# Seven block products for the forget-gate and value projections of a hybrid attention and recurrence block, in a phase of their own

## The chip, the cores and the metric

The kernel runs on one core of a Trainium2 chip. The metric is the device time of one execution in microseconds; the runs give a median. A core has several engines with a queue each: PE multiplies matrices (its weight loads are shown as PEld), DVE works on vectors, ACT evaluates functions, POOL does small jobs, and SP mostly issues transfers. Each engine takes its instructions in a fixed order and waits at one whose inputs are not ready.

## The reference, cut to what matters

One block works on 256 tokens `x` and 256 context tokens `ctx`, 2048 wide. All 512 tokens are normalised and modulated, and go through one wide projection `w_in`. Its columns feed an attention branch and a recurrence branch (16 heads of 128), which are gated, merged and projected out.

```python
xn = rmsnorm(h, norm_gain[l]) * (1.0 + scale) + shift
cn = rmsnorm(hc, norm_gain[l]) * (1.0 + scale_c) + shift_c
aq, ak, av, ag, hq, hff, hfb, hi, hg, ma, mb = split_columns(xn @ w_in[l])
caq, cak, cav, cag, chq, chff, chfb, chi, chg, cma, cmb = split_columns(cn @ w_in[l])
...
def hgrn_forget(z, lb):
    f = lbf + (1.0 - lbf) * jax.nn.sigmoid(z.astype(jnp.float32))
    return to_heads(jnp.log(f)), to_heads(1.0 - f)
...
g_f, k_f = hgrn_forget(hff, lb_f_all[l]);  g_b, k_b = hgrn_forget(hfb, lb_b_all[l])
cg_f, ck_f = hgrn_forget(chff, lb_f_all[l]);  cg_b, ck_b = hgrn_forget(chfb, lb_b_all[l])
v_h = to_heads(hi);  cv_h = to_heads(chi);  q_h = to_heads(jax.nn.silu(hq))
s_f = hgrn2_final_state(ck_f, cv_h, cg_f)                     # the context's state, and backward
o, _, _ = hgrn2_bidir(q_h, v_h, k_f, g_f, k_b, g_b, s_f, s_b)  # forward and backward recurrence
hg_branch = hgrn_readout(o, hgrn_norm_gain[l], hg)            # rmsnorm per head, times silu(hg)
...
y = sigmoid(m_a + b_m[0]) * (hg_branch @ w_o_hgrn) + sigmoid(m_b + b_m[1]) * (att_branch @ w_o_attn)
h = h + gate * (y @ w_out)
```

The forget gates (`hff`, `hfb`) and the values (`hi`) are needed for all 512 tokens, as are the attention's keys and values; the other columns for the 256 tokens of `x` alone.

## The kernel before, in words

**Projections.** Everything is float32. A product is made of three: the weights and the tokens are split into a high part in a shorter format and the rest, and `mm3` (L83 to L85) adds high × high, high × rest and rest × high. `xH` and `xL` hold the split tokens, transposed: 16 slices of 128 features by 512 tokens. A weight chunk of 512 KB is loaded by SP into `raw` (four buffers, L66), copied by ACT to `wh` (L76) and subtracted by DVE into `wl` (L77), three buffers of each. Such a chunk feeds 12 or 24 matmuls, and it is the unit in which a projection is handed out. `proj_col_g` gives 256 columns of weights, transposed, for 512 tokens (a forget gate of two heads: 96 matmuls of 512 columns); `proj_tok_g` gives 512 columns for two or four tiles of 128 tokens (values: four tiles, 192 matmuls of 512); `proj_col_x_g` gives the recurrence's queries.

**Recurrence.** The 16 heads are done as eight pairs by `pair`, a generator. It starts with scans over the forget gates (DVE L525, L526, L529), goes through the levels of products inside the tokens (`A`, `al`, `grow`, `keep`), and ends thus: PE makes `al` (L711), DVE makes the end states from it (L716), PE makes `ob` (L728 to L730), ACT squares it (L736), POOL takes the root (L181, L182), DVE multiplies by gate and root (L740), and PE transposes the result as `to` (L748). These last transposes are put off into the next pair (`done`); ahead of them the next pair's scans are already written down. `X` is a single buffer that both pairs use.

**The order.** PE's order is written out by hand. `weave` takes from a filler of projection steps as much as each `yield` of the pair asks for: 8.5 steps of 24 matmuls in all, and lets the filler run to its end before the next pair. The filler of pair n is `inputs(n + 1)`: the next pair's forget gates, values, output gate and queries; that of the last pair is three merge projections. `with_gates` adds one gate chunk (`gate_chunk`: a 512 KB load of `w_ada`, two L196 on DVE into the sum `acc`) for each three steps of 24 matmuls of filler. There are four groups of eight, each ended by transposes on PE (`tqg`, L202) and a reduction on DVE (L204), all into the same `acc`; what is not yet done after the last pair is done by a loop of 33 steps. Next come `part_a` (the recurrence's output projection, `w_o_hgrn`) and the attention, with its K and V projections. SP's queue has its loads in the order in which the program asks for chunks. DVE, ACT and POOL are ordered by a scheduler from priorities.

Of the kernel before, what the change touches and what calls it, by code (L numbers as in the profile page):

```python
# [7 lines left out]
F32 = mybir.dt.float32  # L8
F32R = mybir.dt.float32r
# [29 lines left out]
def block_kernel(ctx: ExitStack, tc: tile.TileContext, x, c, cx, c_ctx, w_ada, b_ada, norm_gain, w_in,  # L39
# [167 lines left out]

    def forget(banks, d, h0, F):
        for i in range(2):
            sg = base.tile([P, 512], F32, tag="sm", name="sg", bufs=3)  # L210
            act.activation(sg, banks[i], AF.Sigmoid)
            dve.tensor_scalar(F[:, i, :], sg, lbc[:, 2 + d, h0 + i: h0 + i + 1],
                              lbc[:, d, h0 + i: h0 + i + 1], op0=ALU.mult, op1=ALU.add)
# [2 lines left out]
    cg = pad.tile([P, KT], F32, name="cg")  # L216
    gcol = few.tile([P, KT], F32, name="gcol")
    gate_rows = dram.tile([KT, P], F32, name="gate_rows")

    FIRST = (("F0", 2), ("F1", 1), ("F0", 2))  # L220
    with pl("st", reuse_waits="tile") as st:
# [249 lines left out]
                    if i == 3 and u + 1 < len(UNITS):  # L471
                        first_loads(u + 1, *UNITS[u + 1])
        with tc.manual_schedule(engines={mybir.EngineType.PE, mybir.EngineType.SP}):
            first_f = [fp.tile([P, 2, 512], F32, tag=tg, name="ff", bufs=nb) for tg, nb in FIRST]
            with tc.high_priority(2 * PRIO):
                for b, (d, h0) in enumerate(((0, 0), (1, 0), (0, 2))):
                    forget(first[b], d, h0, first_f[b])
            hi = proj_tok_g(w_in, C_HI, x_st, range(4))
            bv0 = result(hi)
# [3 lines left out]
        dve.tensor_copy(mk.rearrange("p a b -> p (a b)"), mkf)  # L483

    biases = {}

# [294 lines left out]
                next(filler, None)  # L781
        run(filler)

    def token_values(bv, grp):
        v = hp.tile([P, 2, 512], F32, tag="v", name="v")
        vc = hp.tile([P, 2, 512], F32, tag="vc", name="vc")
        for t in range(4):
            to_, from_ = (v if t < 2 else vc)[:, t % 2, :], bv[t]
            if t % 2:
                dve.tensor_copy(to_, from_)  # L790
            else:
                act.activation(to_, from_, AF.Copy)
        grp[:2] = [v, vc]

    def output_gate(bg, grp):
        grp[2] = hp.tile([P, 2, 512], F32, tag="gate", name="gate")
        for t in range(2):
            sg = base.tile([P, 512], F32, tag="sm", name="sgg", bufs=3)
            act.activation(sg, bg[t], AF.Sigmoid)
            dve.tensor_tensor(grp[2][:, t, :], bg[t], sg, op=ALU.mult)  # L800

    def gates():

# [12 lines left out]
        while True:  # L816
            yield

    def inputs(n, grp, res):

        g, p = divmod(n, 2)
        h0 = 2 * n
        if n == 1:

            output_gate((yield from proj_tok_g(w_in, C_HG, x_st, range(2))), grp)
        F = [first_f[2] if h0 == 2 and d == 0 else
             fp.tile([P, 2, 512], F32, tag=f"F{d}", name=f"F{d}", bufs=2 - d) for d in range(2)]
        if h0 > 2:
            forget((yield from proj_col_g(w_in, C_FF + h0 * HD)), 0, h0, F[0])
        forget((yield from proj_col_g(w_in, C_FB + h0 * HD)), 1, h0, F[1])  # L830
        if p == 0:
            bv = yield from proj_tok_g(w_in, C_HI + 512 * g, x_st, range(4))
            token_values(bv, grp)
            output_gate((yield from proj_tok_g(w_in, C_HG + 512 * g, x_st, range(2))), grp)
        res[:] = [F, (yield from proj_col_x_g(w_in, C_HQ + h0 * HD))]

    def with_gates(filler):

        for got in filler:
# [2 lines left out]
                count[0] -= 3 * STEP  # L842
                next(gate)
            yield got

    def merge_inputs():
        for n in range(3):
            bm = yield from proj_tok_g(w_in, C_MA + n * 512, x_st, range(2))
            y[n] = fp.tile([P, 2, 512], F32, tag="F0" if n < 2 else "F1", name="y", bufs=2 if n < 2 else 1)
            merge_gate(bm, n, 0, y[n])  # L850

    y = [None] * 4

    def merge_gate(bm, n, row, dst):
        bb = biases.pop((row, n), None)
        if bb is None:
            bb = bias_row(row, n)
        for t in range(2):
            dve.tensor_tensor(dst[:, t, :], bm[t], bb, op=ALU.add)
            act.activation(dst[:, t, :], dst[:, t, :], AF.Sigmoid)  # L860

    with tc.manual_schedule(engines={mybir.EngineType.PE}):
# [3 lines left out]
        token_values(bv0, grps[0])  # L866
        res = [first_f[:2], None]
        res[1] = result(proj_col_x_g(w_in, C_HQ))
        for n in range(8):
            if n == 7:  # L870
                for m in range(2):
                    biases[0, m] = bias_row(0, m, res[0][0][:, 0, 0:1])
# [21 lines left out]
    y[3] = hp.tile([P, 2, 512], F32, tag="vc", name="y")  # L894
    merge_gate(bm, 3, 0, y[3])
    for n in range(1, 4):
        part_a(n)

    XH, XL = xH[:, :, T:], xL[:, :, T:]

    def k_mov(j):
        return XH[:, 2 * j: 2 * j + 2, :], XL[:, 2 * j: 2 * j + 2, :]
# [5 lines left out]
    def split(dh, dl, src, **kw):  # L910
        act.activation(dh, src, AF.Copy, **kw)
        dve.tensor_tensor(dl, src, dh.bitcast(F32), op=ALU.subtract)

    sgb = {}
    Q_TAGS = (("v", "qk"), ("gate", "so"))
# [8 lines left out]
    with tc.manual_schedule(engines={mybir.EngineType.PE}):  # L924
# [1 line left out]
        pool.tensor_copy(sk[:, 0:1], gcol[:, 0:1])  # L926
        nc.gpsimd.dma_start(sk, row_bcast(sink, 16))

        def rope(dst, src, t):

            cos = cs[:, K_COS + t * HD: K_COS + (t + 1) * HD].unsqueeze(1).to_broadcast([P, 4, HD])
            dve.tensor_tensor(dst, src.rearrange("p (h d) -> p h d", h=4), cos, op=ALU.mult)
            tmp = base.tile([P, 4, 2, 2, 32], F32, tag="bb", name="rt", bufs=2)
            sv = src.rearrange("p (h a s d) -> p h a s d", h=4, a=2, s=2)
            sn = cs[:, K_SIN + t * HD: K_SIN + (t + 1) * HD].rearrange("p (a s d) -> p a s d", a=2, s=2)
            for s in range(2):
                dve.tensor_tensor(tmp[:, :, :, s, :], sv[:, :, :, 1 - s, :],
                                  sn[:, :, s, :].unsqueeze(1).to_broadcast([P, 4, 2, 32]), op=ALU.mult)
            tf = tmp.rearrange("p h a s d -> p h (a s d)")
            dve.tensor_tensor(dst, dst, tf, op=ALU.add)  # L940


        bk = proj_tok(w_in, C_K, x_st, range(4))
        kr = at.tile([P, 4, 4, HD], F32, tag="A", name="kr")
        for t in range(4):
            if t < 2:
                rope(kr[:, t], bk[t], t)
            else:
                act.activation(kr[:, t], bk[t].rearrange("p (h d) -> p h d", h=4), AF.Copy)
        bv = proj_tok(w_in, C_V, x_st, range(4))  # L950
        for t in range(4):
            rows = slice(8 + 2 * t, 10 + 2 * t)
            split(XH[:, rows, :], XL[:, rows, :], bv[t].rearrange("p (r c) -> p r c", r=2))

        def keys():
            for z in range(2):
# [142 lines left out]
    for n in range(4):  # L1099
        part_b(n)  # L1100
        if n < 3:
            sgn = gt_tile(n + 1, [P, 2, 512], "sgb")
            merge_gate(sgb[n + 1], n + 1, 1, sgn)
            sgb[n + 1] = sgn
        if n < 2:
            sgb[n + 2] = proj_tok(w_in, C_MB + (n + 2) * 512, x_st, range(2))


    def y_st(kt, t):
# [131 lines left out]
```

## Time and profile before

| | us |
|---|---|
| median of three runs (lowest, highest) | 1630.77 (1630.21, 1631.41) |
| span of the profiled execution | 1629.5 |
| PE busy | 1610.9 |
| PE weight loads busy | 1328.6 |
| DVE busy | 938.3 |
| ACT busy | 762.4 |
| POOL busy | 36.9 |
| mean DMA rate over the span | 168 GB/s |

The span goes from the first to the last instruction of one execution; 1.3 us lie between it and the median. Busy times of different engines overlap. In a row of a group stand line, engine, operation, output and inputs, shape, count, then busy time and mean of one in ns, and the idle time of its engine just before, with what ended it. In a row of the timeline stand start and length in us, and in brackets the idle time before it. In a row of a window stand its ends, then busy time and count of PE, weight loads, DVE, ACT and POOL, the granted PE clock, the DMA engines' busy share and GB/s.

### The profile page before, as it was taken

Reading aid. Unit: us, or ns where it says so; the run is one execution under the profiler, and the core shown is the slowest. Engines: PE = TensorE matmul, PEld = TensorE weight load, DVE = VectorE, ACT = ScalarE, POOL = GpSimd, SP = SyncE. Lnnn points to the kernel's source line nnn. Section 1 sums busy time; section 2 is a strip of 40 time slices with the busy share of each in tenths; the row PEclk is TensorE's granted clock in tenths of the full one; section 3 lists DMA queues with packets and bytes.
Section 4 is the critical chain, followed back from the end, with each engine's and each line's share of the span. In section 5 each row is a group of like instructions: output and inputs, shape, how many; then the busy total and the mean of one; then the engine's idle time right before and its main releaser. Section 6 shows DMA issues by size and latency. Waiting matters only on the chain.

```text
span 1629.5 us, 24667 instructions
## 1 busy us (share of the span) xinstructions
PE 1610.9 (99%) x9882; PEld 1328.6 (82%) x9882; DVE 938.3 (58%) x1464; ACT 762.4 (47%) x1200; POOL 36.9 (2%) x94
## 2 busy tenths in 40 slices
PE   7999999999999999999999999999999999999998
PEld 4668888888888888888888888888888888788887
DVE  4444567546664466645666455335677676555764
ACT  4333455424543345424456443224586786454542
POOL 2000000000000000000000000000000000000000
PEclk9999999999999999999999999999999999999999
DMA  9993544345344553435345555324544454666652
GB/s 368 386 359 129 154 144 143 105 144 189 96 129 130 159 165 104 143 104 188 110 127 171 183 194 194 128 91 145 178 143 143 136 168 155 232 215 205 208 194 91
DMA packets 186690, 274.88 MB, mean 169 GB/s; under 512 B 8624, under 2 KB 105296, under 8 KB 185808
## 3 DMA queue, kind: packets, MB, share of 16 engines
q1 hardware_dynamic: 184032, 266.85, 50.1%
q0 software_dynamic: 1824, 5.35, 1.1%
q8 instruction: 77, 1.26, 0.3%
q10 hardware_dynamic: 720, 1.11, 0.2%
q14 instruction: 37, 0.30, 0.1%
HBM read 271.17 MB, written 2.11 MB: 168 GB/s over the span
## 4 chain that ended last, share of the span: by engine, by line
PE 97%; DVE 1%; issue 1%; ACT 0%; DMA 0%; POOL 0%; POOLq 0%; SPq 0%; ACTq 0%
PE pj L83 24%; PE pj L85 24%; PE pj L84 24%; PE pj L141 7%; PE pj L146 4%; PE pj L409 2%; PE pa L305 2%; PE al L589 1%; PE pj L403 1%; PE pf L409 1%; PE sb L670 1%; PE tkp L1031 1%; PE oba L83 0%; DMA X<-in_x_dram 0%; PE sc L85 0%
## 5 line engine op out<-in xcount | busy, mean ns | idle before, releaser
L77 DVE TENSOR_TENSOR wl<-raw,wh 128x1024 fp32r<-128x1024 f32 x384 | 469.2, 1223 | 400.8 <-ACT wh L76 400.3
L76 ACT ACTIVATE wh<-raw 128x1024 fp32r<-128x1024 f32 x384 | 406.4, 1059 | 581.6 <-PE pj L85 422.1
L84 PE MATMUL pj<-wl,xHL 128*128 128x512 f32 (+1 forms) x1024 | 395.7, 387 | 0.4 <-DVE wl L77 0.4
L85 PE MATMUL pj<-wh,xHL 128*128 128x512 f32 (+1 forms) x1024 | 395.6, 386 | 0.0
L83 PE MATMUL pj<-wh,xHL 128*128 128x512 f32 (+1 forms) x1024 | 391.8, 390 | 0.0
L85 PEld LDWEIGHTS pj<-wh,xHL 128*128 128x128 f32 x1024 | 192.4, 188 | 39.1
L84 PEld LDWEIGHTS pj<-wl,xHL 128*128 128x128 f32 x1024 | 192.6, 188 | 38.2 <-DVE wl L77 0.7
L83 PEld LDWEIGHTS pj<-wh,xHL 128*128 128x128 f32 x1024 | 192.4, 188 | 38.2 <-DVE yt L1087 0.4
L141 PE MATMUL pj<-xHL,wh 128*128 128x512 f32 x512 | 181.1, 396 | 0.0
L83 PE MATMUL pj<-xHL,wh 128*128 128x512 f32 x416 | 164.8, 396 | 0.0
L85 PE MATMUL pj<-xHL,wl 128*128 128x512 f32 x416 | 162.3, 390 | 0.0
L84 PE MATMUL pj<-xHL,wh 128*128 128x512 f32 x416 | 162.1, 390 | 0.0
L146 PE MATMUL pj<-xHL,wl 128*128 128x256 f32 x512 | 139.9, 283 | 0.0
L141 PEld LDWEIGHTS pj<-xHL,wh 128*128 128x128 f32 x512 | 95.1, 188 | 19.1
L84 PE MATMUL pj<-wl,bH 128*128 128x512 f32 x256 | 99.9, 390 | 0.0
L85 PE MATMUL pj<-wh,bL 128*128 128x512 f32 x256 | 99.7, 389 | 0.0
L146 PEld LDWEIGHTS pj<-xHL,wl 128*128 128x128 f32 x512 | 96.7, 189 | 2.5
L85 PEld LDWEIGHTS pj<-xHL,wl 128*128 128x128 f32 x416 | 78.1, 188 | 16.6
L84 PEld LDWEIGHTS pj<-xHL,wh 128*128 128x128 f32 x416 | 78.2, 188 | 15.5
L83 PEld LDWEIGHTS pj<-xHL,wh 128*128 128x128 f32 x416 | 78.2, 188 | 15.5
L83 PE MATMUL pj<-wh,bH 128*128 128x512 f32 x256 | 90.0, 390 | 0.1
L635 DVE TENSOR_TENSOR A<-A,X 128x512 f32<-128x512 f32 x96 | 61.9, 686 | 16.7 <-ACT qk L565 6.7
(289 smaller groups left out, 1690.8 us busy)
## 6 DMA issues: line engine op xcount, KB each, us to landing
raw<-in_w_in_dram SPq DMA_DIRECT2D x300, 512.0 KB, 3.5
raw<-in_w_ada_dram SPq DMA_DIRECT2D x96, 512.0 KB, 7.2
raw<-in_w_o_hgrn_dram SPq DMA_DIRECT2D x32, 512.0 KB, 3.5
raw<-in_w_o_attn_dram SPq DMA_DIRECT2D x32, 512.0 KB, 4.3
raw<-in_w_out_dram SPq DMA_DIRECT2D x28, 512.0 KB, 4.3
X<-in_x_dram SPq DMA_DIRECT2D x2, 1024.0 KB, 6.6
X<-in_ctx_dram SPq DMA_DIRECT2D x2, 1024.0 KB, 10.7
raw<-in_w_in_dram SPq DMA_DIRECT2D x8, 256.0 KB, 7.2
```

The lines of the kernel that those rows point to most:

```text
L76: act.activation(h[:, :n], raw[:, :n], AF.Copy)
L77: dve.tensor_tensor(lo[:, :n], raw[:, :n], h[:, :n].bitcast(F32), op=ALU.subtract)
L83: pe.matmul(o, s[0], m[0], start=first, stop=False)
L84: pe.matmul(o, s[0], m[1], start=False, stop=False)
L85: pe.matmul(o, s[1], m[0], start=False, stop=last)
L141: pe.matmul(banks[i].rearrange("p (a t) -> p a t", a=2), h[:, j, cs_], xHL[:, :, kt, :T], start=kt == 0, stop=kt == KT - 1)
L146: pe.matmul(banks[i][:, :T], lo[:, j, cs_], xH[:, kt, :T], start=False, stop=False)
L305: pe.matmul(pa[32 * g: 32 * g + 32, : 2 * w], cT[:, k0 + g, :], rv_[:, :, g, :], start=k0 == 0, stop=k0 == KT - 4, tile_position=(0, 32 * g))
L403: pe.matmul(o, hw, xL[:, kt, :], start=False, stop=last)
L409: pe.matmul(p_[0], p_[1 + z], xH[:, kt, :], start=kt == 0 and z == 0, stop=False)
L589: pe.matmul(o, ky, mv, start=True, stop=True, tile_position=(0, 32 * g))
L635: dve.tensor_tensor(av, av, f.unsqueeze(3).to_broadcast([P, 2, n2, b]), op=ALU.mult)
```

## The change: a phase ahead of the recurrence

The projection of 2048 features to some columns for 512 tokens is taken as a product of two-by-two blocks: features in two halves, tokens in two halves (of `x` and of the context), weight columns in two halves. By Winograd's form of Strassen's scheme it needs seven block products instead of eight, with sums of blocks on either side. The sums of tokens are made once (`token_sums`, into `S`); the differences of weight blocks are made by DVE for each quad of blocks (`combos`: four subtractions), and seven blocks instead of four are split into `wh` and `wl`. A quad of forget columns (`quad_col`, 13 of them) has 7 × 24 matmuls of 256 columns, a quad of value columns (`quad_tok`, three) 2 × 7 × 24. The partial sums are put together in PSUM, by ACT copies and DVE additions. The first three forget projections and the first value projection stay as they were.

The results are written to device memory by POOL's queue (`F_dr`, `v_dr`), and each pair loads its own. Beside the pairs now run other projections: output gates, seven merge and attention projections (`side_work`; `SIDE` says how many chunks go to each pair) and the queries of the next pair. What they make goes to device memory too, and is loaded at `part_a` and in the attention. After the change a line number of the kernel is higher by 216 in the recurrence (L711 becomes L927, L740 L956, L748 L964).

```diff
+        def combos(b):
+            t = tmp()
+            yield b["11"]
+            sub(t, b["12"], b["11"]);  yield t
+            sub(t, b["22"], t);  yield t
+            yield b["22"]
+            sub(b["12"], b["22"], b["12"]);  yield b["12"]
+            yield b["21"]
+            sub(t, b["21"], t);  yield t
...
+        def quad_col(d, h0):
+            co = (C_FF, C_FB)[d] + h0 * HD
+            b = {n: wload(w_in, 1024 * (n[0] == "2"), 8, (co + HD * (n[1] == "2"),), HD)[0]
+                 for n in ("11", "12", "22", "21")}
+            m_ = [bank8()[:, :T] for _ in range(3)]
+            into = {0: (0, True), 1: (1, True), 2: (0, False), 3: (1, False), 4: (0, False), 5: (2, True), 6: (0, False)}
...
+            for (i, _, mv), src in zip(ORDER, combos(b)):
+                h, lo = [a.rearrange("p (k c) -> p k c", k=8) for a in two(src)]
...
+                    pe.matmul(o, h[:, k, :], mh, start=fresh and k == 0, stop=False, skip_group_check=True)
+                    pe.matmul(o, h[:, k, :], ml, start=False, stop=False, skip_group_check=True)
...
+                    pe.matmul(o, lo[:, k, :], mh, start=False, stop=k == 7,
...
+            nc.gpsimd.dma_start(F_dr[d][h0 // 2], F.rearrange("p i t -> p (i t)"))
...
+            bv0 = proj_tok(w_in, C_HI, x_st, range(4))
...
+            for g in range(2):
+                token_sums(g)
+            for n in range(1, 8):
+                for d in range(2):
+                    if (d, n) != (0, 1):
+                        quad_col(d, 2 * n)
+            for g in range(1, 4):
+                quad_tok(C_HI + 512 * g, v_dr[g])
...
+        for step in ((output_gate(1), merge_out(0, 0), output_gate(2)), (attn_keys(),),
+                     (merge_out(0, 1), output_gate(3), merge_out(0, 2)),
+                     (merge_out(0, 3), merge_out(1, 2), merge_out(1, 3)), (attn_values(),)):
...
+    SIDE = (13, 14, 9, 13, 14, 13, 14, 9)
...
-            weave(pair(n // 2, n % 2, grps[n // 2], *res),
-                  with_gates(inputs(n + 1, grps[(n + 1) // 2], nxt) if n < 7 else merge_inputs()))
+            weave(pair(n // 2, n % 2, grps[n // 2], *res), with_gates(inputs(n, nxt)))
...
-    part_a(0)
-    bm = proj_tok(w_in, C_MA + 3 * 512, x_st, range(2))
+        nc.gpsimd.dma_start(y[n].rearrange("p t c -> p (t c)"), ma_dr[n])
+    for n in range(4):
         part_a(n)
```

Three places show how the instructions move. The first is PE at the end of the last pair. `ob` is the pair's output, `to` its transposes, `tqg` those of a gate group, and `pj` a projection (of `xHL`, the tokens, or of `bH`, the recurrence's output). Before:

```order
L730 MATMUL ob<-so,A 128x128
L728 MATMUL ob<-v,X_7406 128x128
L729 MATMUL ob<-X_7406,A 128x128
L730 MATMUL ob<-so,A 128x128
L83 MATMUL pj<-wh,xHL 128x512
L84 MATMUL pj<-wl,xHL 128x512
L85 MATMUL pj<-wh,xHL 128x512
L83 MATMUL pj<-wh,xHL 128x512
```

And after:

```order
L944 MATMUL ob<-v,X_10559 128x128
L945 MATMUL ob<-X_10559,A 128x128
L946 MATMUL ob<-so,A 128x128
L964 MATMUL to<-cs,so 128x128 x4
L202 MATMUL tqg<-cs,acc 128x128 x4
L83 MATMUL pj<-wh,bH 128x512 x2
L84 MATMUL pj<-wl,bH 128x512
L85 MATMUL pj<-wh,bL 128x512
```

Before, a projection of the tokens follows `ob`, and `to` comes 84 matmuls later; after, `to` and `tqg` follow at once, and then the output projection, which needs them.

The second is SP's queue of loads about the same time. Before:

```order
L66 DMA raw<-in_w_in_dram 128x2x512 x2
L66 DMA raw<-in_w_in_dram 128x4x256 x4
L66 DMA raw<-in_w_ada_dram 128x2x512
L66 DMA raw<-in_w_in_dram 128x4x256 x12
L66 DMA raw<-in_w_in_dram 128x2x512 x24
L66 DMA raw<-in_w_o_hgrn_dram 128x2x512 x8
```

And after:

```order
L66 DMA raw<-in_w_in_dram 128x2x512 x3
L66 DMA raw<-in_w_ada_dram 128x2x512
L66 DMA raw<-in_w_in_dram 128x2x512 x3
L66 DMA raw<-in_w_ada_dram 128x2x512 x11
L66 DMA raw<-in_w_o_hgrn_dram 128x2x512 x32
```

The last gate chunk stood 36 loads of `w_in` ahead of the output projection's weights; now eleven stand in a row right ahead of them.

The third is DVE where one pair ends and the next begins: scans of the next pair, then the product for `so` (that is, for `to`). Before, from the fifth pair to the sixth:

```order
L525 SCALAR_TENSOR_TENSOR X_5670<-F_5052,zero 128x255
L526 SCALAR_TENSOR_TENSOR X_5670<-F_5053,zero 128x255
L529 SCALAR_TENSOR_TENSOR X_5670<-F_5052,X_5670 128x512
L529 SCALAR_TENSOR_TENSOR X_5670<-F_5053,X_5670 128x512
L540 TENSOR_TENSOR qk<-A 128x512
L740 SCALAR_TENSOR_TENSOR so<-ob,ss,gate 128x128 x4
L77 TENSOR_TENSOR wl<-raw,wh 128x1024 x2
```

And after:

```order
L741 SCALAR_TENSOR_TENSOR X_9289<-F_8986,zero 128x255
L742 SCALAR_TENSOR_TENSOR X_9289<-F_8987,zero 128x255
L745 SCALAR_TENSOR_TENSOR X_9289<-F_8986,X_9289 128x512
L745 SCALAR_TENSOR_TENSOR X_9289<-F_8987,X_9289 128x512
L756 TENSOR_TENSOR qk<-A 128x512
L956 SCALAR_TENSOR_TENSOR so<-ob,ss,gate 128x128 x4
L753 TENSOR_TENSOR qk<-qk,hsum 128x256
L196 SCALAR_TENSOR_TENSOR acc<-raw,cg,acc 128x512
```

DVE's order is the same at this place; what stands on PE between `ob` and `to` is not: at this boundary (from the fifth pair to the sixth) 72 matmuls of projection before, 12 after.

More of the change, by code (lines that the diff above doesn't have):

```diff
@@ L473, in block_kernel @@
         with tc.manual_schedule(engines={mybir.EngineType.PE, mybir.EngineType.SP}):
[L474 to L479, printed above, removed]
+            for b, (d, h0) in enumerate(((0, 0), (1, 0), (0, 2))):
+                tg, nb = FIRST[b]
+                ff = fp.tile([P, 2, 512], F32, tag=tg, name="ff", bufs=nb)
+                with tc.high_priority(2 * PRIO):
+                    forget(first[b], d, h0, ff)
+                nc.gpsimd.dma_start(F_dr[d][h0 // 2], ff.rearrange("p i t -> p (i t)"))
             nc.sync.dma_start(cs[:, P:], cst[:, P:])
@@ L799, in output_gate, with merge_out, rope, split @@
             act.activation(sg, bg[t], AF.Sigmoid)
-            dve.tensor_tensor(grp[2][:, t, :], bg[t], sg, op=ALU.mult)
+            dve.tensor_tensor(sg, bg[t], sg, op=ALU.mult)
+            nc.gpsimd.dma_start(hg_dr[g][:, t * 512: (t + 1) * 512], sg)
+    def merge_out(row, n):
+        bm = yield from proj_tok_g(w_in, (C_MA, C_MB)[row] + n * 512, x_st, range(2))
+        bb = bias_row(row, n)
+        for t in range(2):
+            sg = base.tile([P, 512], F32, tag="sm", name="sgm", bufs=3)
+            dve.tensor_tensor(sg, bm[t], bb, op=ALU.add)
+            act.activation(sg, sg, AF.Sigmoid)
+            nc.gpsimd.dma_start((ma_dr, mb_dr)[row][n][:, t * 512: (t + 1) * 512], sg)
+    def rope(dst, src, t):
+        cos = cs[:, K_COS + t * HD: K_COS + (t + 1) * HD].unsqueeze(1).to_broadcast([P, 4, HD])
+        dve.tensor_tensor(dst, src.rearrange("p (h d) -> p h d", h=4), cos, op=ALU.mult)
+        tmp = base.tile([P, 4, 2, 2, 32], F32, tag="bb", name="rt", bufs=2)
+        sv = src.rearrange("p (h a s d) -> p h a s d", h=4, a=2, s=2)
+        sn = cs[:, K_SIN + t * HD: K_SIN + (t + 1) * HD].rearrange("p (a s d) -> p a s d", a=2, s=2)
+        for s in range(2):
+            dve.tensor_tensor(tmp[:, :, :, s, :], sv[:, :, :, 1 - s, :],
+                              sn[:, :, s, :].unsqueeze(1).to_broadcast([P, 4, 2, 32]), op=ALU.mult)
+        tf = tmp.rearrange("p h a s d -> p h (a s d)")
+        dve.tensor_tensor(dst, dst, tf, op=ALU.add)
+    XH, XL = xH[:, :, T:], xL[:, :, T:]
+    def split(dh, dl, src, **kw):
+        act.activation(dh, src, AF.Copy, **kw)
+        dve.tensor_tensor(dl, src, dh.bitcast(F32), op=ALU.subtract)
+    def attn_keys():
+        bk = yield from proj_tok_g(w_in, C_K, x_st, range(4))
+        for t in range(4):
+            kr_ = base.tile([P, 512], F32, tag="sm", name="kr", bufs=3)
+            if t < 2:
+                rope(kr_.rearrange("p (h d) -> p h d", h=4), bk[t], t)
+            else:
+                act.activation(kr_, bk[t], AF.Copy)
+            nc.gpsimd.dma_start(k_dr[:, t * 512: (t + 1) * 512], kr_)
+    def attn_values():
+        bv = yield from proj_tok_g(w_in, C_V, x_st, range(4))
+        for t in range(4):
+            rows = slice(8 + 2 * t, 10 + 2 * t)
+            split(XH[:, rows, :], XL[:, rows, :], bv[t].rearrange("p (r c) -> p r c", r=2))
     def gates():
@@ L817, in gates, with load_forgets, side_work, inputs @@
             yield
[L819 to L835, printed above, removed]
+    def load_forgets(n):
+        F = [fp.tile([P, 2, 512], F32, tag=f"F{d}", name=f"F{d}", bufs=2 - d) for d in range(2)]
+        for d in (1, 0):
+            nc.gpsimd.dma_start(F[d].rearrange("p i t -> p (i t)"), F_dr[d][n])
+        return F
+    def side_work():
+        for step in ((output_gate(1), merge_out(0, 0), output_gate(2)), (attn_keys(),),
+                     (merge_out(0, 1), output_gate(3), merge_out(0, 2)),
+                     (merge_out(0, 3), merge_out(1, 2), merge_out(1, 3)), (attn_values(),)):
+            for g in step:
+                yield from g
+                yield 0
+    side = side_work()
+    SIDE = (13, 14, 9, 13, 14, 13, 14, 9)
+    def inputs(n, res):
+        units, F = 0, None
+        for _ in range(SIDE[n]):
+            got = next(side, None)
+            if got is None:
+                break
+            units += got
+            if F is None and n < 7 and units >= 4 * STEP:
+                F = load_forgets(n + 1)
+            yield got
+        if n < 7:
+            F = F or load_forgets(n + 1)
+            res[:] = [F, (yield from proj_col_x_g(w_in, C_HQ + 2 * (n + 1) * HD))]
+        else:
+            run(side)
     def with_gates(filler):
@@ L844, in with_gates @@
             yield got
[L846 to L850, printed above, removed]
     y = [None] * 4
@@ L927, in block_kernel @@
         nc.gpsimd.dma_start(sk, row_bcast(sink, 16))
[L929 to L943, printed above, removed]
-        kr = at.tile([P, 4, 4, HD], F32, tag="A", name="kr")
[L945 to L953, printed above, removed]
+        kr = at.tile([P, 4, 4, HD], F32, tag="A", name="kr")
+        nc.gpsimd.dma_start(kr.rearrange("p t h d -> p (t h d)"), k_dr)
         def keys():
@@ L1102, in block_kernel @@
             sgn = gt_tile(n + 1, [P, 2, 512], "sgb")
-            merge_gate(sgb[n + 1], n + 1, 1, sgn)
+            if n == 0:
+                merge_gate(sgb[1], 1, 1, sgn)
+            else:
+                nc.gpsimd.dma_start(sgn.rearrange("p t c -> p (t c)"), mb_dr[n + 1])
             sgb[n + 1] = sgn
-        if n < 2:
-            sgb[n + 2] = proj_tok(w_in, C_MB + (n + 2) * 512, x_st, range(2))
     def y_st(kt, t):
```

198 lines of the change are left out of this document (175 added, 23 removed).

## The prediction

> **What bounds the kernel now.** I read the page's busy shares and slices first, then its chain of waits, then the costliest groups.
>
> ```profile
> span 1629.5 us, 24667 instructions
> PE 1610.9 (99%) x9882; PEld 1328.6 (82%) x9882; DVE 938.3 (58%) x1464; ACT 762.4 (47%) x1200; POOL 36.9 (2%) x94
> PE   7999999999999999999999999999999999999998
> DVE  4444567546664466645666455335677676555764
> PEclk9999999999999999999999999999999999999999
> ...
> PE 97%; DVE 1%; issue 1%; ACT 0%; DMA 0%; POOL 0%; POOLq 0%; SPq 0%; ACTq 0%
> ...
> L77 DVE TENSOR_TENSOR wl<-raw,wh 128x1024 fp32r<-128x1024 f32 x384 | 469.2, 1223 | 400.8 <-ACT wh L76 400.3
> ```
>
> PE is the bound from end to end: 99% busy, full in every slice but the first and the last, and 97% of the chain. DVE is at 58%, and its largest group waits for others. So PE time that the change removes comes off one for one, and so does every stall that it adds; there is hardly one to be removed. The span is 1629.5 us and the median of the runs 1630.77, so I add 1.3 us to a span.
>
> **The saving on PE.** A busy time is no pitch, since matmuls overlap. The pitch is read from starts in the timeline of PE, in two unbroken stretches (the first and last row of 24 intervals, then of 23):
>
> ```profile
> 1579.65 0.62 PE L83 MATMUL pj<-wh,xHL 128*128 128x512 f32 x2
> ...
> 1585.09 0.62 PE L83 MATMUL pj<-wh,xHL 128*128 128x512 f32 x2
> ...
> 1599.16 0.28 PE L83 MATMUL pj<-wh,xHL 128*128 128x256 f32 x1
> ...
> 1601.92 0.28 PE L83 MATMUL pj<-wh,xHL 128*128 128x256 f32 x1
> ```
>
> The pitch is 5.44/24 = 226.7 ns at 512 columns and 2.76/23 = 120.0 ns at 256. In the rows of PE's order the change takes 1824 matmuls of 512 columns away and adds 3192 of 256: 1824 × 0.2267 − 3192 × 0.1200 = 413.5 − 383.0, or 30.4 us less. Seven eighths of the arithmetic would have saved more; narrow matmuls give a part of it back, 13.3 ns each over half of the wide one.
>
> [...]
>
> **The ends of the pairs.** Each pair of heads ends in ob, whose results go through squares (ACT), a root (POOL) and a product (DVE L740), and back to PE for the transposes to (L748). DVE has the next pair's scans ahead of that product, and they can't start before ob, since X is one buffer. In the timeline (PE's last ob, then DVE without a gap):
>
> ```profile
> 439.45 0.39 PE L730 MATMUL ob<-so,A 128*128 128x128 f32 x2
> 439.66 0.69 DVE L525 TENSOR_TENSOR_SCAN X<-F,zero 128x255 f32<-128x255 f32 x1
> ...
> 442.00 1.26 DVE L529 SCALAR_TENSOR_TENSOR X<-F,X 128x512 f32<-128x512 f32 x2
> 443.19 0.68 DVE L540 TENSOR_TENSOR qk<-A 128x512 f32<-128x512 f32 x1
> 443.79 1.12 DVE L740 SCALAR_TENSOR_TENSOR so<-ob,ss,gate 128x128 f32<-128x128 f32 x4
> ```
>
> The product ends at 444.91, 5.2 us after ob was done (no later than 439.66, when DVE could start). Before, 11 to 76 us of projection stood on PE between ob and to, so nobody noticed. After, PE's order has 12 matmuls of 512 (12 × 0.2267 = 2.72 us) there at four of the seven boundaries, 24 (5.44 us) at two, 48 at one. PE is in order, so the transposes hold the projection behind them. Stall: 5.2 − 2.72 = 2.5 us, up to 2.9 where a split stands on DVE ahead of the scans, four times 2.7; about 0.6 at the two; none at the last: **+12 us** (10 to 16; it can't be a gain). The projections that stood there are the very ones now done earlier, so no other work takes their place.
>
> **The end of the recurrence.** In the last pair nothing at all is left on PE between al, ob and to. The last pair before, in the timeline, with the group of the gate's chunks and the loads:
>
> ```profile
> 889.01 1.12 DVE L716 SCALAR_TENSOR_TENSOR X<-so,X,al 128x128 f32<-128x128 f32 x4 [0.45 <-PE al L711]
> ...
> 896.72 0.39 PE L730 MATMUL ob<-so,A 128*128 128x128 f32 x2
> 897.14 0.28 ACT L736 ACTIVATE so<-ob 128x128 f32<-128x128 f32 x1 [1.57 <-PE ob L730]
> ...
> 899.72 1.12 DVE L740 SCALAR_TENSOR_TENSOR so<-ob,ss,gate 128x128 f32<-128x128 f32 x4 [2.89 <-POOL ss L182]
> ...
> L196 DVE SCALAR_TENSOR_TENSOR acc<-raw,cg,acc 128x512 f32<-128x512 f32 x60 | 44.9, 748 | 45.8 <-DMA raw<-in_w_ada_dram 45.1
> ...
> raw<-in_w_o_hgrn_dram SPq DMA_DIRECT2D x32, 512.0 KB, 3.5
> ...
> L76 ACT ACTIVATE wh<-raw 128x1024 fp32r<-128x1024 f32 x384 | 406.4, 1059 | 581.6 <-PE pj L85 422.1
> ```
>
> ob waits for L716, 0.45 + 1.12 = 1.5 us after al; to waits for L740, 900.84 − 897.1 = 3.7 us after ob. Then comes what the shorter pairs leave over. Gate chunks are paid out by projection time in the pairs, which is now less: by the order 21 of 32 are done in them, 11 at the end, and SP's queue has all 11 ahead of the first w_o_hgrn weights. acc is one sum, so the eight chunks of the last group start only when the transposes tqg of the group before are over. Each is two L196 of 0.75 us, start to start some 0.67, so 1.34 us; L204 (0.7) goes first. With four raw buffers the first w_o_hgrn load gets that of the fifth chunk: 0.7 + 5 × 1.34 = 7.4 us after tqg, landing 3.5 us later, split on ACT 1.06, and on DVE behind most of the chunks 1.2: PE goes on about 13 us after tqg. The sum is 1.5 + 3.7 + 13.2 = **18.4 us** (14 to 22); before, PE had 196 us of projection there and the chunks long done.
>
> A gap can also cost the clock behind it. After this kernel's own first idle time, the windows (PE, weight loads, DVE, ACT, POOL, granted clock, DMA share, GB/s) show 0.84 and then 0.59:
>
> ```profile
> 18.00:21.00 3.00, 1.66 (x9) 1.30 (x9) 1.61 (x9) 0.03 (x1) 2.38 (x6) 0.84 1.09 385
> 21.00:24.00 3.00, 3.00 (x17) 1.27 (x16) 0.00 (x0) 0.00 (x0) 0.13 (x1) 0.59 1.09 386
> ```
>
> The two stretches are 0.5 and 1.2 us short of full clock, 1.7 us for a long gap, which I leave to the range. [...]
>
> **The new phase.** PE needs 168 × 0.12 = 20.2 us for a forget block. DVE does seven splits, four differences, three sums and two scalings for it:
>
> ```profile
> L1137 DVE TENSOR_TENSOR lw<-lw,gt 128x1024 f32<-128x1024 f32 x4 | 4.9, 1226 | 4.3 <-DMA lw<-in_w_out_dram 4.3
> L156 DVE TENSOR_TENSOR hsum<-pj,hsum 128x256 f32<-128x256 f32 x32 | 13.3, 415 | 0.0
> L212 DVE TENSOR_SCALAR F<-sg,lbc 128x512 f32<-128x512 f32 x26 | 14.1, 544 | 30.4 <-ACT sg L211 30.4
> raw<-in_w_in_dram SPq DMA_DIRECT2D x300, 512.0 KB, 3.5
> 265.00:310.00 45.00, 45.00 (x460) 37.66 (x459) 26.38 (x46) 19.98 (x38) 0.00 (x0) 1.00 0.34 106
> 920.00:960.00 40.00, 40.00 (x178) 33.14 (x177) 19.76 (x18) 15.38 (x15) 0.00 (x0) 1.00 0.60 194
> ```
>
> 11 × 1.225 + 3 × 0.415 + 2 × 0.544 = 15.8 us, under 20.2. A chain remains: block 12 keeps its buffer until its difference is split, then comes the reload, a difference, a split, and a bank that must be read out before product seven writes it. With a landing of 3.5 us I reckon some 1 us of slack. The blocks come in pieces of 512 bytes, which this trace hardly shows. From the two windows, 1 KB pieces (a forget projection) move 106/0.34 = 312 GB/s over 16 engines, 52 ns a piece, and 2 KB pieces 323 GB/s, 101 ns; on that line 512 bytes take some 28 ns, so a load (64 pieces an engine) is no slower. If they cost 52 ns, it takes 64 × 0.052 − 32 × 0.052 = 1.7 us longer: 22 us in 13 blocks. The nearest row is the line's own lower end, so I take the first, with **+4 us** for the starts and the value blocks' halves (0 to 22). The token sums, 43 us of DVE beside 43.5 us of the first value projection on PE, get **+1 us** (0 to 5). The stores and reloads go through POOL, 2% busy, some 90 issues of 0.6 to 0.8 us, and the reloads stand a pair ahead: nothing, while each is covered by a pair's 50 us.
>
> **The pairs themselves.** The last pair before had only 12-matmul chunks beside it, as all have after:
>
> ```profile
> 829.00:895.00 66.00, 66.00 (x582) 56.06 (x581) 48.82 (x78) 41.48 (x74) 3.08 (x8) 1.00 0.54 166
> ```
>
> DVE is busy for 48.8 of 66 us, and PE has no stall. A pair after is some 53 us on PE; 13 us fewer are 4.8 chunks with a split of 1.22 each, so DVE has 48.8 − 5.8 = 43 of 53 us, 81% instead of 74%. The wait that can come is on L196 or a level product late by a split. Nearest is this row, without a stall; the far bound is DVE at 51 of 53 with its chain exposed for 2 to 3 us a pair. I take **+5 us** (0 to 20). K, V and merge projections moved into the pairs keep their matmuls; y, kr and the gates come from memory by loads issued long before: nothing.
>
> **Sum.** −30.4 + 12 + 18.4 + 4 + 1 + 5 = +10.0 us: span 1639.5, median about 1640.8. I forecast 1640. About 0.2%, 3.3 us, is what a measurement tells from no change.
>
> **Rivals.**
> - The tail is short: the last eight gate chunks cost PE nothing, because w_o_hgrn's weights get buffers before them. Then 13.2 us fall away: −3.2, 1627.5, and faster with any other term at its lower end (no wait in the phase: 1623). It decides when the tail's stall is under 5 us. Against it: SP's order has the chunks first, and L196's row shows that DVE takes them at 0.75 us each.
> - Small pieces cost as much as 1 KB ones: +18 on top, 1658. For it: nothing in the trace shows the line going on below 1 KB.
> - DVE bounds the pairs: 20 instead of 5, 1655. For it 81% in a mean; against it the pair without a stall at 74%.
> - Narrow matmuls lose less than the two stretches say, as where each issue costs next to nothing beyond its columns: with the wide pitch simply halved, 113 ns, 51.7 us are saved and not 30.4, 1619. Against it are the 23 equal intervals of 120 ns.
> - That the saving isn't made is no case: the 1824 and 3192 stand in PE's order.
>
> **Chances.** Forecast case (stalls at ends and boundaries as counted) 0.57, short tail 0.12, small pieces 0.13, DVE 0.15, pitch 0.03. Faster: most of the short tail (0.08), the pitch (0.03), and 0.08 of the forecast case with its terms at their lower ends (10 + 14 + 0 + 0 + 0 − 30.4 = −6) make 0.19. Same: 0.03 of the short tail and 0.08 of the forecast case, 0.11. Slower: 0.70. The range goes from 1624, the short tail, to 1662, one of the large bounds with some of the other.
>
> **What the profile after would show.** A pitch of 120 ns in the phase, 20.2 us from one forget block to the next (22 or more: pieces or chain); gaps of 2.5 to 3 us on PE ahead of to at four boundaries, released by DVE's product; one idle time of about 13 us after the last tqg, ended by a weight split; PE's share down to 97%. Wrong if the last is missing, if the boundaries show no gap, or if the gaps in the pairs add up to more than both.

## The result: 2.2% slower, 1666.6 us

| | us |
|---|---|
| before, median (lowest, highest) | 1630.71 (1630.21, 1631.41) |
| after, median (lowest, highest) | 1666.61 (1664.88, 1667.80) |
| ratio, 95% interval | 1.0219 (1.0205 to 1.0233) |
| span of the profiled execution, before and after | 1629.5 and 1666.0 |

The page of the changed kernel, the rows that answer to those shown of before:

```profile
span 1666.0 us, 28103 instructions
PE 1599.0 (96%) x11250; PEld 1379.5 (83%) x11250; DVE 1142.8 (69%) x1677; ACT 844.0 (51%) x1317; POOL 83.6 (5%) x183
...
PE   7999999999999998989989999969999999999998
...
PEclk9999999999999999999999999979999999999999
...
PE 84%; DVE 7%; DMA 4%; issue 2%; ACT 2%; POOL 0%; SPq 0%; POOLq 0%; DVEq 0%; ACTq 0%
...
raw<-in_w_in_dram SPq DMA_DIRECT2D x300, 512.0 KB, 3.6
```

PE is still the bound, but it is no longer full: slices 16 to 27, which are the recurrence and its end, have holes, and one slice has a lower clock. The phase ahead of them has none. Its blocks end at even distances, as the stores of POOL's timeline show, and PE is busy for all of a stretch in it (window: PE, weight loads, DVE, ACT, POOL, clock, DMA share, GB/s):

```profile
299.68 0.53 POOL L627 DMA_DIRECT2D F<-F  x1 [19.63 <-DVE F L625]
319.85 0.53 POOL L627 DMA_DIRECT2D F<-F  x1 [19.63 <-DVE F L625]
...
320.00:340.00 20.00, 20.00 (x169) 20.00 (x169) 15.16 (x16) 9.49 (x13) 0.38 (x1) 1.00 0.43 133
```

20.16 to 20.17 us a block is 168 × 0.120 us: by the phase's pitch the saving on PE came in full. The loads in pieces of 512 bytes stall nothing: the 48 that were issued between 200 and 440 us landed in 3.6 us (median), as did those of the whole tensor, and PE has no wait in the phase. Where the time went is in the list of what PE waited for (sum, count, longest):

```profile
PE to L964 <- DVE so L956: 23.4, 12, 5.0
PE pj L83 <- ACT wh L76: 15.4, 1, 15.4
...
PE tqg L202 <- DVE bL L970: 4.1, 2, 2.9
PE ob L946 <- DVE X L932: 2.3, 3, 1.2
```

Each is a wait at a pair's end or in the tail (from the last pair's `al` on). Before, the same list has no wait ahead of `to`, `tqg`, `ob` or the output projection, and none above 0.5 us behind the kernel's first 35 us. But the waits, 25.6 us at the seven pair ends and 19.6 in the tail, are not all that is lost there. PE's timeline at the fifth pair end:

```profile
905.36 0.33 PE L964 MATMUL to<-cs,so 128*128 128x128 f32 x1 [2.04 <-DVE so L956]
905.88 0.90 PE L964 MATMUL to<-cs,so 128*128 128x128 f32 x3 [0.19 <-DVE so L956]
906.43 0.78 PE L83 MATMUL pj<-wh,xHL 128*128 128x512 f32 x1
907.01 0.63 PE L84 MATMUL pj<-wl,xHL 128*128 128x512 f32 x1
907.43 0.63 PE L85 MATMUL pj<-wh,xHL 128*128 128x512 f32 x1
...
909.68 0.39 PE L85 MATMUL pj<-wh,xHL 128*128 128x512 f32 x1
909.91 0.39 PE L83 MATMUL pj<-wh,xHL 128*128 128x512 f32 x1
```

After this gap of 2 us matmuls start 0.43 us apart, not 0.23, for some 3 us. The windows show it as a granted clock below 1 at this pair end and in the tail (before, it is 1.00 in every stretch of 20 us from 40 to 1620 us):

```profile
900.00:920.00 20.00, 17.77 (x88) 14.72 (x87) 17.07 (x32) 11.85 (x25) 2.58 (x8) 0.91 0.44 136
1080.00:1120.00 40.00, 21.25 (x84) 16.46 (x84) 23.46 (x34) 11.30 (x20) 2.34 (x4) 0.70 0.64 212
```

I measured each pair end from the start of ob to the next `tw` (PE's transposes of the next pair's scans), less what its matmuls take unhindered (ob 2.6 us, a projection by its 0.2267 us, to 0.45), and the slow stretch after tw where one is left: 6.4, 7.7, 3.3, 6.3, 4.3, 5.6, 6.0 us, 39.6 in all; of these 25.6 are waits and 14 slow matmuls. The tail, from al to the second tqg, took 1107.36 − 1075.21 = 32.2 us for 7.6 us of matmuls: 24.6 lost, 19.6 waiting and 5 slow. With −30.4 for the blocks and 1 us of waits inside the pairs that makes +34.8; the spans differ by 36.5. Of the other 1.7 us, 1.0 stands already in the first 62 us, where PE waits somewhat longer for its first loads (the `pa` that starts at 60.64 us before starts at 61.63 us after); the rest is not placed.

### The profile page after: what moved, and what is told of

Same layout as the page of the kernel before. It is cut to its first block, busy times and chain, and to the rows that moved or that the text cites. A ratio compares the mean times of both kernels' runs of the same rounds, so it can differ in the third digit from the quotient of the medians.

```text
span 1666.0 us, 28103 instructions
## 1 busy us (share of the span) xinstructions
PE 1599.0 (96%) x11250; PEld 1379.5 (83%) x11250; DVE 1142.8 (69%) x1677; ACT 844.0 (51%) x1317; POOL 83.6 (5%) x183
## 4 chain that ended last, share of the span: by engine, by line
PE 84%; DVE 7%; DMA 4%; issue 2%; ACT 2%; POOL 0%; SPq 0%; POOLq 0%; DVEq 0%; ACTq 0%
PE pj L83 14%; PE pj L84 13%; PE pj L85 13%; PE pj L141 5%; DMA raw<-in_w_ada_dram 3%; PE pj L601 3%; PE pj L597 3%; PE pj L596 3%; PE pj L146 3%; PE pm L601 3%; PE pm L597 3%; PE pm L596 3%; PE pj L415 2%; DVE wl L77 2%; PE pa L311 2%
## 5 line engine op out<-in xcount | busy, mean ns | idle before, releaser
L83 PE MATMUL pj<-wh,xHL 128*128 128x512 f32 (+1 forms) x832 | 325.3, 396 | 0.0
L84 PE MATMUL pj<-wl,xHL 128*128 128x512 f32 (+1 forms) x832 | 323.7, 389 | 0.0
L85 PE MATMUL pj<-wh,xHL 128*128 128x512 f32 (+1 forms) x832 | 323.0, 388 | 0.0
L85 PEld LDWEIGHTS pj<-wh,xHL 128*128 128x128 f32 x832 | 158.1, 190 | 32.5
L83 PEld LDWEIGHTS pj<-wh,xHL 128*128 128x128 f32 x832 | 158.5, 191 | 30.8 <-ACT sg L211 0.4
L141 PE MATMUL pj<-xHL,wh 128*128 128x512 f32 x512 | 180.9, 395 | 0.0
L141 PEld LDWEIGHTS pj<-xHL,wh 128*128 128x128 f32 x512 | 95.0, 188 | 18.6
L83 PE MATMUL pj<-wh,bH 128*128 128x512 f32 x256 | 92.3, 397 | 15.5 <-ACT wh L76 15.4
L146 PEld LDWEIGHTS pj<-xHL,wl 128*128 128x128 f32 x512 | 96.6, 189 | 3.2 <-DVE wl L77 0.7
L577 ACT ACTIVATE wh<-T 128x1024 fp32r<-128x1024 f32 x57 | 60.3, 1058 | 74.3 <-DVE T L558 22.8
L578 DVE TENSOR_TENSOR wl<-T,wh 128x1024 fp32r<-128x1024 f32 x57 | 69.6, 1220 | 17.6 <-ACT wh L577 17.6
L83 PEld LDWEIGHTS pj<-wh,bH 128*128 128x128 f32 x256 | 48.6, 191 | 26.7 <-ACT wh L76 15.8
L196 DVE SCALAR_TENSOR_TENSOR acc<-raw,cg,acc 128x512 f32<-128x512 f32 x60 | 44.9, 749 | 36.6 <-DMA raw<-in_w_ada_dram 35.9
```

The source lines that it names most:

```text
L83: pe.matmul(o, s[0], m[0], start=first, stop=False)
L84: pe.matmul(o, s[0], m[1], start=False, stop=False)
L85: pe.matmul(o, s[1], m[0], start=False, stop=last)
L141: pe.matmul(banks[i].rearrange("p (a t) -> p a t", a=2), h[:, j, cs_], xHL[:, :, kt, :T], start=kt == 0, stop=kt == KT - 1)
L146: pe.matmul(banks[i][:, :T], lo[:, j, cs_], xH[:, kt, :T], start=False, stop=False)
L577: act.activation(h, src, AF.Copy)
```

## The experiments

Theory 1: the loss is PE waiting for DVE at the pair ends and for the gate chunks in the tail. Theory 2, which goes with it: the gaps also cost slow matmuls. The main rivals: DVE is simply too busy in the recurrence, so that moving one wait makes another; the reloads from device memory delay things; the seven products don't save what they should. Each ran against the kernel before on the same chip, whose median was 1630.65 both times.

**The put-off transposes later.** `e1_to_after_tw` moves three lines of `pair`.

```diff
-        for f in done:
-            f()
-        done[:] = []
         yield 0.5
         wT = X2[:, 1024:].rearrange("p (a s) -> p a s", a=8)
...
         yield 1.0
+        for f in done:
+            f()
+        done[:] = []
         so = hp.tile([P, 2, 512], F32, tag="so", name="so")
```

> The put-off transposes `to` stand after the next pair's `tw` and 24 more matmuls, just ahead of sb. Theory 1 (PE waits at the pair ends for DVE's product, and each such gap also lowers the clock): at the seven pair ends of the changed kernel some 39 us are lost; now `tw` is what PE waits for, and only the two ends whose scans are behind a gate chunk still wait. About 14 us stay lost there, the tail stays as it is: 1666.6 - 26 = 1641 us (1633 to 1650), and hardly a wait of PE `to`. Rival (DVE is short of time in the pairs, so its lateness shows up at whatever comes next, tw or sb): within 5 us of 1666.6.

Measured: 1641.3 us (1639.6 to 1642.3), ratio 1.0062 (1.0047 to 1.0077). What PE waits for now:

```profile
PE pj L83 <- ACT wh L76: 15.7, 1, 15.7
...
PE tw L872 <- DVE X L745: 6.4, 3, 2.8
PE to L964 <- DVE so L956: 3.3, 2, 3.1
```

The 23.4 us of `to` are 3.3 (those of the tail), and 6.4 are at tw at the second and seventh pair end. 25 us came back: DVE is late at the pair ends, not short of time in the pairs, and the rival falls.

**The gate chunks in the phase.** `e2_gates_in_phase` loads them into the idle buffer of F1, one ahead of and one within each forget block, the last six within the value blocks, and sums the four groups in the two halves of acc in turn.

```diff
-        wr = wload(w_ada, k0 * P, 2, (4096 + 512 * g,), 512)[1][:, 0]
+        wr = fp.tile([P, 2, 512], F32, tag="F1", name="gr", bufs=1)
+        nc.sync.dma_start(wr, w_ada[k0 * P: (k0 + 2) * P, 4096 + 512 * g: 4608 + 512 * g]
...
+        def pay():
+            if paid[0] < 32:
+                g, k = divmod(paid[0], 8)
+                gate_chunk(accT[:, g % 2, :], g, 2 * k)
+                paid[0] += 1
...
-            weave(pair(n // 2, n % 2, grps[n // 2], *res), with_gates(inputs(n, nxt)))
+            weave(pair(n // 2, n % 2, grps[n // 2], *res), inputs(n, nxt))
```

> All 32 gate chunks are taken in the phase ahead of the recurrence, into a buffer of their own (the one of F1, idle there), two a block; none is left in the pairs or the tail. Theory 1 with the gate chunks as the reason of the tail (25 us lost with the slow clock behind it) and of the long waits at the second and the seventh pair end: the tail loses 2 us instead of 25, the pair ends about 18 less, the phase at most 6 more: 1627 us (1618 to 1640). Rival (the reloads from device memory, not the chunks, make DVE late at the pair ends): only the tail is saved, 1643 us.

Measured: 1634.9 us (1631.1 to 1637.1), ratio 1.0023 (1.0014 to 1.0033). PE's waits:

```profile
PE to L980 <- DVE so L972: 9.6, 8, 2.4
...
PE pj L608 <- DVE sg L626: 5.6, 5, 2.6
PE pj L608 <- ACT wh L579: 3.2, 2, 2.2
```

The 15.4 us wait of the tail is gone, and so are the waits ahead of `to` at the second and the seventh pair end; what is left is 2.0 to 2.4 us at four pair ends, just the ends with 12 matmuls. In exchange the phase, with 1.34 us more on DVE for each chunk, stalls for some 11 us. The reloads are all still there, so the rival (1643) falls too; the time alone, half way between the two forecasts, would not show it, the waits do.

The edit changed more than I had written: PE's order in the tail is another. The output projection of the finished heads now stands between the last pair's ob and to:

```profile
1070.94 0.39 PE L961 MATMUL ob<-so,A 128*128 128x128 f32 x2
1071.08 0.48 PE L83 MATMUL pj<-wh,bH 128*128 128x512 f32 x1
...
1086.35 0.40 PE L83 MATMUL pj<-wh,bH 128*128 128x512 f32 x1
1086.58 0.27 PE L980 MATMUL to<-cs,so 128*128 128x128 f32 x1
```

So the tail's 0.9 us ahead of ob and 3.3 us ahead of to went as well. The same order stands in `e6_chunks_in_pairs`, `e12_both`, `e15_spread` and `e16_no_phase_chunks`, whose tails have no gate chunks either.

Why a chunk made a pair end longer is seen in DVE's timeline of the changed kernel, at the second one (ob is done at 709.5):

```profile
710.12 0.41 DVE L753 TENSOR_TENSOR qk<-qk,hsum 128x256 f32<-128x256 f32 x1
714.03 0.75 DVE L196 SCALAR_TENSOR_TENSOR acc<-raw,cg,acc 128x512 f32<-128x512 f32 x1 [3.51 <-DMA raw<-in_w_ada_dram]
714.70 0.68 DVE L741 TENSOR_TENSOR_SCAN X<-F,zero 128x255 f32<-128x255 f32 x1
...
719.82 1.12 DVE L956 SCALAR_TENSOR_TENSOR so<-ob,ss,gate 128x128 f32<-128x128 f32 x4
```

DVE stands for 3.5 us at a gate chunk whose load has not landed, with the scans and the product for `to` behind it. PE had 24 matmuls here, and still waited 5.0 us.

**The clock by itself.** `e3_keep_warm` puts transposes of the identity, whose results nobody reads, ahead of each `to`.

```diff
+            warm = ps.tile([P, 512], F32, tag="tp", name="warm")
+            for q in range(24):
+                pe.transpose(warm[:, (q % 4) * P: (q % 4 + 1) * P], ident, ident)
             to = ps.tile([P, 2, 2, HD], F32, tag="tp", name="to")
```

> 24 idle transposes of the identity stand ahead of each `to`, some 2.6 us of PE at full clock; nobody reads them. Theory 2 (a gap of 2 to 5 us on PE costs as much again as slow matmuls after it, some 2.2 us at each pair end): the gaps are filled by work of no use, the waits for DVE stay, and 12 us of slow clock fall away: 1654 us (1648 to 1660), with the granted clock near 1.00 behind the first seven pair ends. Rival (the clock falls for another reason, such as the load itself): no gain, 1666 to 1672, clock as low as now.

Measured: 1656.7 us (1655.8 to 1657.1), ratio 1.0156 (1.0139 to 1.0173): 10 us less with 192 instructions more. The windows around the fifth pair end and the seventh:

```profile
900.00:920.00 20.00, 20.00 (x223) 16.85 (x222) 14.73 (x26) 11.86 (x18) 1.70 (x3) 1.00 0.68 211
...
1010.00:1030.00 20.00, 19.94 (x117) 17.74 (x115) 15.36 (x31) 9.75 (x23) 1.99 (x6) 0.92 0.41 134
```

The clock is 1.00 in the windows at the first six pair ends (at the third it was so already); at the seventh it still falls, to 0.92, where PE waits 2.4 us in ob, ahead of the idle work. At the other five, where the changed kernel's windows have 0.91 or 0.92, the gap, once filled, no longer lowers it: there it was the gap that did.

But a gap doesn't always do it. In the changed kernel and in `e4_plain_phase` (below) PE waits the same 2.94 us ahead of the same tqg, at the third pair end; the 6 us behind it, in the one and in the other:

```profile
791.38:797.38 6.00, 6.00 (x33) 5.17 (x34) 3.52 (x9) 3.49 (x6) 1.32 (x2) 1.00 0.59 174
...
819.03:825.03 6.00, 6.00 (x21) 5.25 (x22) 2.99 (x8) 2.39 (x5) 1.32 (x2) 0.51 0.62 177
```

In `e2_gates_in_phase` two gaps of 2.05 us ahead of to were followed by 1.00 (at 670 us) and by 0.72 (at 907 us). In the recurrences of these runs a single gap of 0.8 to 1.8 us left the clock at 0.98 to 1.00 in the 6 us behind it, and each of 3 us or more lowered it (in the changed kernel 3.21 us to 0.72, 4.03 to 0.72, 5.03 to 0.61, 15.41 to 0.50); between, neither length nor place decides, and what does stays open.

**The seven products undone.** `e4_plain_phase` keeps the phase, the stores and the reloads, and makes the blocks with `proj_col_g` and `proj_tok` (eight block products, no token sums).

```diff
-                        quad_col(d, 2 * n)
+                        banks = result(proj_col_g(w_in, (C_FF, C_FB)[d] + 2 * n * HD))
...
+                            forget(banks, d, 2 * n, F)
...
-                quad_tok(C_HI + 512 * g, v_dr[g])
+                bv = proj_tok(w_in, C_HI + 512 * g, x_st, range(4))
```

> The phase, its stores and reloads, and all else stay, but the 13 forget blocks and three value blocks are made as before by eight block products (matmuls of 512 columns), without the token sums. Theory 1 (the seven products save on PE what was counted): 13 x 1.6 + 3 x 3.2 = 30.4 us more, 1697 us (1693 to 1701). Rival (the narrow matmuls and DVE's extra work eat the saving): at most 10 us more, under 1677.

Measured: 1693.6 us (1688.8 to 1697.7), ratio 1.0383 (1.0361 to 1.0405). 27.0 us more than with seven products, where 30.4 were counted; the highest run is 31 over the changed kernel's median, the lowest 22, so the difference of 3 is not settled. The saving is real. PE's waits, and the busy shares:

```profile
PE to L972 <- DVE so L964: 20.6, 12, 3.8
PE pj L83 <- ACT wh L76: 16.0, 1, 16.0
...
PE 1633.0 (96%) x9882; PEld 1341.0 (79%) x9882; DVE 935.4 (55%) x1464; ACT 763.0 (45%) x1200; POOL 83.2 (5%) x183
```

The waits for `to` and in the tail are there as well, with DVE at 55%: they come with the new order of the recurrence, not with the seven products.

**All chunks in the pairs.** `e6_chunks_in_pairs` changes one number.

```diff
-            if count[0] >= 3 * STEP:
-                count[0] -= 3 * STEP
+            if count[0] >= 15 * STEP // 8:
+                count[0] -= 15 * STEP // 8
```

> Gate chunks are paid out for each 1.875 steps of projection instead of 3, so that all 32 are taken in the pairs; `to` stays where the change has it. Theory 1 (the tail is lost to the chunks that stand in front of w_o_hgrn's weights): the tail's 25 us shrink to about 1; half again as many chunks stand on DVE in the pairs, and where one waits for its load ahead of the scans, a pair end gets longer, 5 us in all: 1648 us (1640 to 1656). Rival (the tail waits for w_o_hgrn's loads themselves or for the last product, whoever stands before them): 1660 or more.

Measured: 1645.8 us (1643.3 to 1648.0), ratio 1.0091 (1.0075 to 1.0108). The tail's wait is gone altogether; PE's wait for `to` is 17.1 us, 7.8 the longest. So the tail's long wait was the chunks in front of w_o_hgrn's weights (here too the output projection moved in between ob and to), and chunks in the pairs make the scans late.

**Together.** `e12_both` is the first two edits; `e15_spread` is the same with one chunk in a forget block, three or four in a value block and the last eight in the pairs; `e16_no_phase_chunks` is the edit of `e1_to_after_tw` with that of `e6_chunks_in_pairs`.

> Both edits together: `to` behind tw, and all gate chunks in the phase. Theory 1: of the kernel with the chunks in the phase (1634.9), the four waits for DVE's product (2.05 + 2.39 + 2.05 + 2.38 = 8.9 us) and the slow clock behind them (about 8 us) fall away; the phase keeps its 10 us of waits for DVE: 1618 us (1612 to 1624), faster than the kernel before. Rival (DVE's lateness moves on to tw, sb or the levels): 1630 or more.

> As both edits, but one gate chunk in a forget block instead of two, four in a value block, and the last eight in the pairs, one for six steps. Theory 1 with DVE's load as what stalled the phase: its waits go from 10 us to about 2, the pairs keep theirs near 0: 1608 us (1602 to 1616). Rival (it is the shared order on SP or the output of a block that stalls the phase, not the number of chunks): 1615 to 1622.

> `to` behind tw, and all 32 gate chunks in the pairs at 1.875 steps each, none in the phase or the tail. Theory 1: 1641.3 of `to` moved alone, less 24 for the tail, plus 3 to 5 for chunks that make the scans late ahead of tw: 1620 us (1614 to 1628). Rival (DVE is now too full in the pairs): 1635 or more.

| | median (lowest, highest) | ratio, interval |
|---|---|---|
| `e12_both` | 1619.6 (1618.3, 1620.2) | 0.9930 (0.9915 to 0.9945) |
| `e15_spread` | 1616.7 (1615.5, 1618.4) | 0.9914 (0.9899 to 0.9929) |
| `e16_no_phase_chunks` | 1628.0 (1620.0, 1635.2) | 0.9980 (0.9965 to 0.9996) |

All are faster than the kernel before, the second by 14 us, the third by an interval that only just leaves out 1. The recurrence of the changed kernel and that of `e15_spread`, in windows (the second runs 14 us into the output projection):

```profile
564.00:1084.00 520.00, 489.16 (x4408) 411.82 (x4407) 371.86 (x620) 288.95 (x540) 50.39 (x111) 0.98 0.61 200
...
600.00:1080.00 480.00, 478.81 (x4424) 407.47 (x4423) 352.86 (x589) 291.50 (x544) 48.20 (x106) 1.00 0.61 198
```

In the second PE is full and the clock is 1.00, with the reloads and the side work as before: DVE isn't short of time there. I had expected 1608 for `e15_spread`. Its remaining waits in the phase, 8.4 us, lie in the first two blocks and one later; the three longest:

```profile
184.16 1.22 PE L616 MATMUL pj<-S,wl 128*128 128x256 f32 x8 [1.34 <-DVE wl L583]
187.58 0.58 PE L611 MATMUL pj<-S,wh 128*128 128x256 f32 x1 [2.20 <-ACT wh L582]
...
224.35 0.35 PE L611 MATMUL pj<-xHL,wh 128*128 128x256 f32 x1 [2.18 <-DVE sg L629]
```

In DVE's order three chunks stand in the first 20 us, where I had written one, next to the last token sums; and `e12_both`, with twice the chunks in a forget block, has the same waits there. So the rival, that the shared order and not the number matters, is the better account; no run took the order alone. `e16_no_phase_chunks` missed by 8 us and its runs spread over 15: half again as many chunks in the pairs make single waits of up to 4.4 us at ob and 2.2 us at tw.

## Why the prediction was wrong

The direction was right, at +36 us instead of +10; the time lies 5 us above the range. The step that failed is the term for the ends of the pairs, with the slow matmuls behind each gap that the sum left out. By the prediction's own terms:

| term | forecast | measured |
|---|---|---|
| saving on PE | −30.4 | −30.4 by the phase's pitch; 27.0 lost when undone |
| ends of the pairs | +12 | +39.6 |
| end of the recurrence | +18.4 | +24.6 |
| new phase | +4 | 0 |
| token sums | +1 | 0 |
| pairs | +5 | +1 |

The last three terms were 9 us too high, which by luck hid a part of what the two ends were short: 27.6 and 6.2 us.

- **The saving** and **the phase**: right. Matmuls of 256 columns start 0.120 us apart (6.7 ns over half of the 226.7 at 512; the 13.3 of the prediction is for two of them), and the slack that I reckoned in a block was enough. The pieces of 512 bytes landed in 3.6 us: the rival of the small pieces is out, and so is that of the cheaper narrow matmuls.
- **The ends of the pairs**: the step that failed. The mechanism was the one named, at the places named, but it was mis-sized by 28 us, in two parts. The waits are 25.6 us instead of 12: I took DVE's 5.2 us from a pair end of before where nothing was in its way. That price holds where no gate chunk is in the pairs: the four ends that still wait in `e2_gates_in_phase` wait 2.0 to 2.4 us each, and 2.5 to 2.9 were forecast. In the changed kernel DVE comes to the scans 1.1 us late at the first end (a split and the sums of the queries' halves stand ahead), 2.1 us late at the fourth (half a gate chunk and a split) and 4 to 5 us late at the second and the seventh, where a gate chunk waits for its load. I had named L196 as a wait that could come, but inside the pairs, at 5 us. The transposes tqg at the third and the sixth pair end wait another 2.9 and 1.1 us, for L970, which I had not seen: they come after `to` in the same PSUM tag and after only 12 matmuls of projection. At the third end 60 matmuls stood ahead of `to`, not 48, and it had no wait.
- **The slow clock**: the other 14 us at the pair ends and 5 in the tail. I had the row for it (0.84 and 0.59 after the first idle time), priced it at 1.7 us for one gap, and left it to the range. Six pair ends and the tail had it. Idle work ahead of `to` took 10 us of it back. The gap ahead of that row was no long one, as I called it: PE had waited 1.5 us, and then 0.3 (in the changed kernel it is 0.8 and 0.3 there, and the clock stays at 1.00). At the pair ends the shortest gaps that slow matmuls followed were 2.04, 2.38 and 2.67 us, at the fifth, the sixth and the first; with idle work ahead of `to` the clock was 1.00 at all three.
- **The end of the recurrence**: the place and the chain were right (0.9, 3.3 and 15.4 us of waits for the 1.5, 3.7 and 13.2 forecast); the 5 us of slow matmuls are what was mainly missing. The rival of a short tail is out.
- **Stores and reloads cost nothing**: PE waits for none of them in the list above, and `e15_spread`, with all of them, has PE full (478.8 of 480 us).
- DVE as the bound of the pairs, a rival at 20 us, is out as such (1 us of waits inside the pairs): what costs is not DVE's load but the order of what stands in its queue.
- The profile after would show a gap "at four boundaries": they are at six, and two of the three longest waits are at the ends with 24 matmuls of cover. One idle time after tqg, ended by a weight split, came as forecast, at 15.4 us instead of 13.

## What to carry to other kernels

Work that is moved away from a place takes its cover along: for each wait that the moved work hid, count the time that is left, from the worst row of the chain and not from a quiet one, and look at what else stands ahead in the waiting engine's queue, loads above all. On PE, price a new gap like those here, 2.0 to 5.0 us, at its length and some 2 us on top, since slow matmuls followed at six of the seven pair ends (14 us in all). And when a good change comes out slower, look for its new gaps: here another place for three lines and for the gate chunks turned +36 us into −14.

## What the runs showed of the hardware that I had not expected

In the changed kernel a gap of 2.0 us on PE was followed by some 3 us of matmuls at 0.43 us instead of 0.23 (906.4 to 909.1 us), and one of 15.4 us by 6 us of them. Of two equal gaps at the same place, 2.94 us, one was followed by a clock of 1.00 and one by 0.51. 192 idle transposes, put into gaps that were there anyway, saved 10 us.
